# Gate blocks of a hybrid encoder layer computed before attention, in pairs with seven block products for eight

## The chip, the cores and the metric

The kernel runs on one core of a Trainium2 chip. A core has five engines that work beside one another, each through its own queue in order: PE (TensorE, matrix products into the accumulators in PSUM), ACT (ScalarE), DVE (VectorE), POOL (GpSimd) and SP, which here issues most transfers between DRAM and the on-chip memory SBUF. The metric is the time of one execution on the chip in microseconds (us); the number to compare is the median of several runs. For the kernel before it is 1957.97 us (three runs, 1956.46 to 1958.05).

## What is computed

One layer of a streaming encoder, for 1024 prompt tokens and 8 x 16 sample tokens together (1152 columns, `NT`). Cut to what matters here:

```python
h = rms_norm(x, norm_g) * (1 + scale) + shift
proj = h @ w_in
q, k, v, z_att, z_ssd, xbc, dt_raw, gates = jnp.split(proj, IN_SPLITS, axis=-1)
...
att_branch = (o_att.reshape(b, s, ATT_WIDTH) * jax.nn.silu(z_att)) @ w_att_proj
...
y = (y + d_skip.astype(jnp.float32)[:, None] * xs_h).reshape(b, s, SSD_WIDTH).astype(x.dtype)
y = y * jax.nn.silu(z_ssd)
...
merged = jax.nn.sigmoid(g_att) * att_branch + jax.nn.sigmoid(g_ssd) * ssd_branch
out = x + gate * (merged @ w_out)
```

All data is float32. `h` is 1024 x 1152 with features on partitions: eight row blocks of 128 (`KT`). A *gate block* is 128 columns of `w_in` for `z_att` (8 blocks) or `z_ssd` (16 blocks) times `h`, followed by a SiLU.

## The kernel before, in words

**Products.** Each float32 operand is split into a rounded high part and the rest (ACT copies to `fp32r`, DVE subtracts, lines 334 and 335 for weights), and a product is three passes: high by high, high by low, low by high. `dense` (line 427, its matmuls on lines 442, 443 and 445) makes one block of 128 outputs in three groups of 384 tokens: 8 row blocks x 3 passes x 3 groups = 72 matmuls of 128x384. `dense_tok` (506 to 508) makes the q, k and v of two heads with tokens on partitions: 9 token tiles of 24 matmuls, 128x384 each. The two accumulators of the pool `psd` (tile `d` in the profile) take turns in both. The attention and scan arithmetic itself runs in small float32 matmuls on other lines.

**Start.** Eight input blocks come in, `h` is normalised and split block by block (for each `k`: ACT lines 646, 651 and 655, DVE lines 633, 642, 643 and 658), and the first gate block is accumulated as each row block of `h` arrives (line 665). Row block `k` of `h` before its split (`ht[k]`) is freed at once.

**Attention.** Eight units of two heads. The dense work of unit u is `dense_tok`, and then the gate block of unit u+1 (line 924). Beside it run, as generators, a `prelude` (q and k are normalised on POOL, lines 960 to 964, and turned by PE, lines 984 and 1000, in three parts: tiles 0 to 3, 4 to 7, 8), and the attention of the unit before (`prompt`: scores on line 1122, DVE 1036, ACT 1031, turns 1043, products with v 1066; `sample`: 1175 to 1212). One buffer `Q` holds the raw q and k of a unit; it is free for the next unit once the third part of the prelude has been turned on line 1000. A token tile's accumulator is read by ACT on 931 and 933, into `Q`, and by DVE on 934.

**Scan (SSD).** Sixteen pairs of heads, p. The dense work of a pair is a convolution block (`conv_gen`), its gate block z (lines 1423 and 1424 read the accumulator), and for ten pairs (`GATED`) a merge gate block (line 1355). Every fourth pair has two convolution blocks more. The scan's own chain (lines 1453 to 1616) runs beside it; the dense work may be two pairs ahead (`AHEAD`).

**Tail.** Merge gates that are left, the two branch projections, the merge and the output projection.

**Order of the work.** Generators of dense work and of the rest are interleaved by `run`: for each piece of dense work its cost times a ratio (0.95 in attention, 0.5 elsewhere) is credit that the rest may spend, and `pause` holds a generator back by a planned time. The instructions so emitted are put into the engines' queues by a scheduler that may take a later instruction when an earlier one is not ready in its own model of time; what is wrapped in `late` stays behind the instruction emitted before it on its engine. At run time each queue is in order.

Of the kernel before, what the change touches and what calls it, by code (L numbers as in the profile page):

```python
# [12 lines left out]
P = 128  # L13
# [18 lines left out]
GATED = (0, 1, 2, 4, 5, 6, 8, 9, 10, 13)  # L32
BIG = -1e30
# [5 lines left out]
FCOLS = COLS - RCOLS - QCOLS - VCOLS  # L39
# [82 lines left out]
def trunk_kernel(ctx: ExitStack, tc: tile.TileContext, h):  # L122
# [12 lines left out]

    class Part:
# [15 lines left out]
    qpart, vpart = Part("q", QCOLS, "left"), Part("v", VCOLS, "right")  # L152
    qarena, varena = qpart.arena, vpart.arena
    q_phase, v_phase = qpart.phase, vpart.phase
    ctx.callback(qpart.close)
    ctx.callback(vpart.close)

    uid = [0]

    def nm(s):  # L160
        uid[0] += 1
        return f"{s}{uid[0]}"
# [40 lines left out]
    Z0 = fixed[0] + 2 * 1024  # L203
    XW = 3 * 288 + 2 * 256
    L_RAW = arena.set_layout(fixed[0], [("raw", 2, 1024)])
    L_ATT = arena.set_layout(Z0, [("Q", 1, 16 * P), ("T", 5, NT), ("S", 10, 640), ("U", 2, 640), ("K", 4, 512), ("q", 1, 256), ("d", 1, 256),
                                  ("k", 1, 128), ("p", 1, 128), ("n", 2, 36 + 3 * 16), ("t", 6, 14)])
    L_ATT["Z"] = L_ATT["T"][2:]
    L_SSD = arena.set_layout(Z0, [("X", 1, XW), ("R", 2, 1184), ("t", 8, 36), ("pad", 1, 576), ("T", 9, NT), ("Y", 1, 1184), ("H", 1, 1024),
                                  ("g", 3, G3)])  # L210
    L_HEAD = dict(L_SSD, T=[x for x in L_SSD["T"] if x[0] + x[1] <= Z0 + 7 * NT])
    L_START = arena.set_layout(Z0, [("T", 11, NT), ("ada", 5, 1024), ("e", 2, 256)])
    L_TAIL = arena.set_layout(Z0, [("T", 15, NT)])
    L_SM = arena.set_layout(Z0 + 15 * NT, [("e", 2, 384)])
# [3 lines left out]
    L_WA = rarena.set_layout(W0, [("w", 2, 1024)])  # L218
# [7 lines left out]
    L_VT = varena.set_layout(0, [("T", 5, 1184)])  # L226
    v_open = [False]

    def alloc(lay, tag, cols, cold=None):
# [12 lines left out]
        if lay is L_W3 or lay is L_W7 or lay is L_VT or lay is L_VA:  # L242
            return Buf(varena, varena.alloc(lay, tag, cols), cols)
        if lay is L_H or lay is L_W or lay is L_WA or lay is L_QR or lay is L_ST:
            return Buf(rarena, rarena.alloc(lay, tag, cols, cold), cols)
# [6 lines left out]
        return Buf(arena, arena.alloc(lay, tag, cols), cols)  # L252

    q_phase("start", F32)
# [14 lines left out]
    x0_ = Z0  # L269
    xv = []  # L270
    for w in (288, 288, 288, 256, 256):
        xv.append(base[:, x0_:x0_ + w])
        x0_ += w
    dt, acs, dtw, dec, decs = xv

# [10 lines left out]
    gate_d = drp.tile([16, P, NT], F32, name="gate_d")  # L286

# [28 lines left out]
    def w_split(i, keep=lambda x: x, cold=None):  # L316

        n = len(jobs[i])
        if n == 4:
            return w_split_last(i, keep)  # L320
        if i not in wsplit:
            lay = L_W3 if n == 3 else L_WA if 0 < i < jobs_att[0] else L_W
# [17 lines left out]
    def w_split_last(i, keep):  # L340
# [6 lines left out]
        if j == 3:  # L347
            row = alloc(L_WA, "w", 1024)
# [68 lines left out]
    job(h["wall"][0])  # L417
    for u in range(NU - 1):
        job(*(h["wall"][1 + 4 * u + i] for i in range(3)))
        job(h["wall"][4 + 4 * u])  # L420
    job(*(h["wlast"][i] for i in range(4)))
    jobs_att = [len(jobs)]
    for x in [h["wall"][i] for i in range(29, 85)] + [h["watt"][i] for i in range(8)] + [h["wssd"][i] for i in range(16)] \
# [3 lines left out]
    def dense(ops, evict, nk=KT, outs=1, last=False, wide=False, order=(0, 1, 2), other=False):  # L427
# [9 lines left out]
        def mm(ps, o, g, k, parts=(0, 1)):  # L437
# [3 lines left out]
            if 0 in parts:  # L441
                nc.tensor.matmul(ps, hi.r[:, wc], kh.r[:, tok], start=k == 0, stop=False)  # L442
                nc.tensor.matmul(ps, hi.r[:, wc], kl.r[:, tok], start=False, stop=False)  # L443
            if 1 in parts:
                nc.tensor.matmul(ps, lo.r[:, wc], kh.r[:, tok], start=False, stop=k == nk - 1)  # L445

        for o in range(outs):
# [21 lines left out]
            for g in order:  # L469
                if g == 2 and att_left[0] == 0:  # L470
# [16 lines left out]
    def dense_tok(evict):  # L487
# [5 lines left out]
        for t in range(9):  # L493

            ps = pg(n) if i == 1 and t == 2 else psd.tile([P, n], F32, tag="d", name=nm("d"))
# [22 lines left out]

    ct_ = alloc(L_START, "e", 256)
    dma(ct_.ap, h["cT"])  # L520
# [1404 lines left out]
```

## Time and profile before

| what | value |
|---|---|
| median of three runs | 1957.97 us (1956.46 to 1958.05) |
| span of the profiled execution | 1955.7 us |
| PE busy | 1938.3 us, 99% of the span |
| DVE, ACT, POOL busy | 1168.5, 776.4, 323.5 us |
| HBM traffic | 192.70 MB read, 43.66 MB written |

The span is from the first to the last instruction; the runs' times are 0.8 to 2.3 us above it, for what lies around it. In a row of the profile stand the line of the kernel, the engine, the operation, what it writes and reads with its shape, and a count; then the busy time, the mean length of one, and the idle time before it with what ended it. In a row of the timeline stand start and length in us first. A matmul's length contains the one behind it in the pipeline, so for PE the distance from start to start is the price of one.

### The profile page before, as it was taken

The numbers are of one execution on the slowest core, as the hardware profiler recorded it, in microseconds if no ns is written. First come the engines' busy times: TensorE is split into PE (matmuls) and PEld (weight loads), VectorE is DVE, ScalarE is ACT, GpSimd is POOL, SyncE is SP. The second block draws the span as 40 slices with busy tenths as digits, with TensorE's granted clock in tenths as the row PEclk, the third lists the DMA queues.
The fourth block names the chain that finished last, engine by engine and source line by source line (L and its number), as shares of the span: only waits on it lengthen the run. The fifth ranks groups of instructions, "written<-read, shape, count | busy, mean of one in ns | idle before, by whom it ended". The sixth has DMA issues, their size and how long they took to land.

```text
span 1955.7 us, 35068 instructions
## 1 busy us (share of the span) xinstructions
PE 1938.3 (99%) x14091; PEld 1859.4 (95%) x14091; DVE 1168.5 (60%) x2441; ACT 776.4 (40%) x1589; POOL 323.5 (17%) x624
## 2 busy tenths in 40 slices
PE   7999999999999999999999999999999999999999
PEld 5999999899998999999999999999999999999999
DVE  7455555556555765757566666576674334777732
ACT  8444444445444557344454434345351301111200
POOL 0312213122131201212212221122212100000000
PEclk9999999999999999999999999999999999999999
DMA  9124244232432325433333333332337642331241
GB/s 367 60 81 131 86 132 131 90 122 88 131 112 96 112 88 160 128 112 110 95 132 129 106 103 114 117 118 91 117 118 291 234 140 92 104 104 56 86 143 52
DMA packets 81209, 238.62 MB, mean 122 GB/s; under 512 B 14284, under 2 KB 15320, under 8 KB 81048
## 3 DMA queue, kind: packets, MB, share of 16 engines
q1 hardware_dynamic: 72088, 207.74, 32.7%
q0 software_dynamic: 8960, 28.65, 3.8%
q8 instruction: 111, 1.82, 0.4%
q14 instruction: 50, 0.41, 0.1%
HBM read 192.70 MB, written 43.66 MB: 121 GB/s over the span
## 4 chain that ended last, share of the span: by engine, by line
PE 96%; DVE 1%; ACT 1%; DMA 1%; issue 0%; SPq 0%
PE d L442 13%; PE d L443 13%; PE d L445 13%; PE s L442 5%; PE s L445 5%; PE s L443 5%; PE d L508 5%; PE d L506 5%; PE d L507 5%; PE g L1043 3%; PE g L1066 3%; PE g L1553 2%; PE s L1122 2%; PE g L1526 1%; PE g L1573 1%; PE g L1122 1%
## 5 line engine op out<-in xcount | busy, mean ns | idle before, releaser
L442 PE MATMUL d<-rarena 128*128 128x384 f32 x1520 | 517.4, 340 | 0.3 <-ACT arena L1355 0.3
L445 PE MATMUL d<-rarena 128*128 128x384 f32 x1520 | 511.4, 336 | 0.0
L443 PE MATMUL d<-rarena 128*128 128x384 f32 x1520 | 511.0, 336 | 0.0
L442 PEld LDWEIGHTS d<-rarena 128*128 128x128 f32 x1520 | 285.6, 188 | 4.6 <-issue 2.3
L443 PEld LDWEIGHTS d<-rarena 128*128 128x128 f32 x1520 | 285.6, 188 | 2.8 <-issue 2.4
L445 PEld LDWEIGHTS d<-rarena 128*128 128x128 f32 x1520 | 285.5, 188 | 1.1 <-issue 0.9
L334 ACT ACTIVATE rarena<-arena 128x1024 fp32r<-128x1024 f32 x92 | 97.5, 1060 | 314.1 <-PE s L443 226.2
L442 PE MATMUL s<-rarena 128*128 128x384 f32 x640 | 216.7, 339 | 0.0
L443 PE MATMUL s<-rarena 128*128 128x384 f32 x640 | 214.2, 335 | 0.0
L445 PE MATMUL s<-rarena 128*128 128x384 f32 x640 | 214.1, 334 | 0.0
L508 PE MATMUL d<-va_att,rarena 128*128 128x384 f32 (+1 forms) x559 | 195.0, 349 | 0.0
L506 PE MATMUL d<-va_att,rarena 128*128 128x384 f32 (+1 forms) x559 | 193.9, 347 | 0.0
L507 PE MATMUL d<-va_att,rarena 128*128 128x384 f32 (+1 forms) x559 | 191.0, 342 | 0.0
L335 DVE TENSOR_TENSOR rarena<-arena,rarena 128x1024 fp32r<-128x1024 f32 x92 | 113.2, 1230 | 82.7 <-ACT rarena L334 82.4
L1031 ACT ACTIVATE arena<-arena 128x640 f32<-128x640 f32 (+2 forms) x144 | 101.4, 706 | 138.0 <-DVE arena L1140 99.7
L442 PEld LDWEIGHTS s<-rarena 128*128 128x128 f32 x640 | 120.3, 188 | 1.0 <-issue 1.0
L443 PEld LDWEIGHTS s<-rarena 128*128 128x128 f32 x640 | 120.3, 188 | 0.0
L445 PEld LDWEIGHTS s<-rarena 128*128 128x128 f32 x640 | 120.1, 188 | 0.0
L508 PEld LDWEIGHTS d<-va_att,rarena 128*128 128x128 f32 x559 | 105.5, 189 | 3.9 <-issue 2.7
L1263 DVE SCALAR_TENSOR_TENSOR arena<-arena 128x1176 f32<-128x1176 f32 x66 | 99.9, 1514 | 15.5 <-ACT arena L1260 14.2
L506 PEld LDWEIGHTS d<-va_att,rarena 128*128 128x128 f32 x559 | 105.2, 188 | 3.1 <-issue 1.2
L507 PEld LDWEIGHTS d<-va_att,rarena 128*128 128x128 f32 x559 | 105.2, 188 | 1.0 <-issue 0.4
(345 smaller groups left out, 3212.9 us busy)
## 6 DMA issues: line engine op xcount, KB each, us to landing
arena<-in_wall_dram SPq DMA_DIRECT2D x85, 512.0 KB, 3.9
arena<-in_kc_dram SPq DMA_DIRECT2D x64, 256.0 KB, 4.2
arena<-in_vc_dram SPq DMA_DIRECT2D x64, 256.0 KB, 3.4
arena<-acs_d SPq DMA_DIRECT2D x19, 576.0 KB, 3.8
gate_d<-arena POOLq DMA_DIRECT2D x48, 192.0 KB, 2.5
arena<-y_d SPq DMA_DIRECT2D x15, 576.0 KB, 5.6
arena<-in_wssd_dram SPq DMA_DIRECT2D x16, 512.0 KB, 4.1
arena<-in_wada_dram SPq DMA_DIRECT2D x15, 512.0 KB, 8.9
```

What stands on the lines that cost most here:

```text
L334: keep(nc.scalar.activation(hi.r[:, c], b.ap, AF.Copy))
L335: keep(nc.vector.tensor_tensor(lo.r[:, c], b.ap, hi.ap[:, c], ALU.subtract))
L442: nc.tensor.matmul(ps, hi.r[:, wc], kh.r[:, tok], start=k == 0, stop=False)
L443: nc.tensor.matmul(ps, hi.r[:, wc], kl.r[:, tok], start=False, stop=False)
L445: nc.tensor.matmul(ps, lo.r[:, wc], kh.r[:, tok], start=False, stop=k == nk - 1)
L506: nc.tensor.matmul(ps, kh.r[:, tok], wh, start=j == 0, stop=False)
L507: nc.tensor.matmul(ps, kh.r[:, tok], wl, start=False, stop=False)
L508: nc.tensor.matmul(ps, kl.r[:, tok], wh, start=False, stop=j == KT - 1)
L1031: nc.scalar.activation(p, p, AF.Exp, bias=sm_[:, 4 + e:5 + e], scale=-1.0, accum_out=sm_[:, 6 + e:7 + e])
L1043: nc.tensor.transpose(ps[:, s * P:(s + 1) * P], p[:, (j + s) * P:(j + s + 1) * P], ident)
L1122: late(nc.tensor.matmul(banks[k][e][:, o:o + w], x.r[hs, qs], y.r[hs, kk], start=i == 0, stop=i == 2))
L1263: nc.vector.scalar_tensor_tensor(yc, r.ap[:, j:j + n], w4[:, i, j:j + 1], yc, ALU.mult, ALU.add)
```

## The change

Seventeen gate blocks (all eight of attention, and those of the scan pairs in `EARLY`) are computed between the start and attention, stored in DRAM (`z_d`), and loaded where they are used. Blocks 0, 1 and 16 are plain. Blocks 2 to 15 are done as seven pairs: two blocks of outputs by two halves of the contraction (even and odd row blocks of `h`) by two halves of the tokens (576 each) are a 2 x 2 block product, made with seven products in Winograd's form of Strassen's identity. The sums of blocks of `h` are made once on POOL, in place (`t_sum`), the sums of blocks of weights for each pair on POOL (`w_form`); both are then split on ACT and DVE. A product is 4 row blocks x 2 groups of 288 tokens x 3 passes. The outputs are summed partly in PSUM, partly by DVE. The memory is cut anew (a pool of 16 slots during this phase, then the arena of attention and scan over the same place). In attention `dense_tok` of unit u+1 follows that of unit u; the ratio there is 1.27. The scan pairs in `EARLY` have no z block of their own.

```diff
+EARLY = (0, 1, 2, 4, 5, 6, 8, 9, 10)
+NZ = 2
+NPR = 7
+TH = NT // 2
+MH = TH // 2
...
+    def t_sum(i, part):
+        a, b = (x.ap.rearrange("p (h c) -> p h c", c=TH) for x in (ht[2 * i], ht[2 * i + 1]))
+        if part == 0:
+            late(nc.gpsimd.tensor_tensor(a[:, 0], a[:, 1], a[:, 0], ALU.subtract))
+            late(nc.gpsimd.tensor_tensor(a[:, 1], b[:, 1], a[:, 1], ALU.subtract))
+        else:
+            late(nc.gpsimd.tensor_tensor(b[:, 1], b[:, 1], a[:, 0], ALU.subtract))
+            late(nc.gpsimd.tensor_tensor(b[:, 0], b[:, 0], b[:, 1], ALU.subtract))
+    def t_split(w, i):
+        x = ht.pop(2 * i + w)
+        hi, lo = thi[w][i], tlo[w][i] = [slots.alloc(F32R) for _ in range(2)]
+        late(nc.scalar.activation(hi.r, x.ap, AF.Copy))
+        late(nc.vector.tensor_tensor(lo.r, x.ap, hi.ap, ALU.subtract))
+        x.free()
+    FORMS = ("P1", "P5", "P7", "P6", "P2", "P4", "P3")
...
+    def w_form():
...
+        tt = lambda out, a, b, op: late(nc.gpsimd.tensor_tensor(out, a, b, op))
+        if f == "P1":
+            tt(t1, part(i1, 0), part(i1, 1), ALU.add)
+            tt(t2, t1, part(i0, 0), ALU.subtract)
+            tt(part(i1, 0), part(i0, 0), part(i1, 0), ALU.subtract)
...
+        late(nc.scalar.activation(v3(w.r[:, hi]), x, AF.Copy))
+        late(nc.vector.tensor_tensor(v3(w.r[:, lo]), x, v3(w.ap[:, hi]), ALU.subtract))
+        if f == "P5":
+            tt(t1, part(i0, 1), t2, ALU.subtract)
...
+        for j, (n, f) in enumerate(seq):
+            while len(forms) < min(j + 4, len(seq)):
+                w_form()
...
+            for i in range(KT // 2):
+                mh, ml, o = mv(i)
+                wh, wl = (w.r[:, c + i * P:c + (i + 1) * P] for c in (0, 512))
+                for g in range(2):
+                    tok = slice(o + g * MH, o + (g + 1) * MH)
+                    late(nc.tensor.matmul(bank[g], wh, mh[:, tok], start=fresh and i == 0, stop=False,
+                                          skip_group_check=not fresh))
...
+            elif f == "P6":
...
+                add(u2.ap, D_, s["p1"].ap)
+                s.pop("p1").free()
+                add(u3.ap, C_, u2.ap)
+                x = o2.ap[:, TH:]
+                add(x, B_, u3.ap)
+                u3.free()
+                silu(x, [v3(x)])
...
     for k in range(KT):
...
-            if 2 < k < 6:
-                w_low2(k - 3)
+            if k == 4:
+                late(nc.vector.tensor_tensor(wsplit[1][1].r, b.ap, wsplit[1][0].ap, ALU.subtract))
...
-        ht.pop(k).free()
...
+        if k % 2:
+            t_sum(k // 2, 0)
+            t_sum(k // 2, 1)
...
+    todo = [0, 1, 2, None, (0, 0), (0, 1), (0, 2), (0, 3), None, (1, 0)]
+    for j, _ in enumerate(dense(hops, ev_z(z[1], late), third=True)):
+        if j % 2 and todo:
+            x = todo.pop(0)
+            if x is None:
+                w_form()
+            elif isinstance(x, int):
+                ev_z(z[0], late)(0, x, groups[x], first[x])
...
+            else:
+                t_split(*x)
...
+    pairs()
+    z = alloc(L_ATT, "T", NT)
+    for i in range(NZ + 2 * NPR, nz):
+        for j, _ in enumerate(dense(hops, ev_z(z))):
+            if j in (6, 9, 12):
+                w_next(i - NPR)
+        dma(z_d[i], z.ap)
...
     def attention(u):
...
             qk = yield from walloc(lay, "Q", 16 * P)
             v = yield from walloc(lay, big, NT)
             nb = yield from walloc(lay, "n", 84)
+            z = zs[u] = yield from walloc(lay, big, NT)
+            dma(z.ap, z_d[u])
...
-                return
-            z = zs[u + 1] = yield from walloc(lay, "Z" if u + 1 == NU - 1 else "T", NT)
-            yield from dense(hops, ev_z(z))
...
-        return dense_gen(), [prelude()], [prompt(), sample()], 0.95
+        return dense_gen(), [prelude()], [prompt(), sample()], 1.27
...
+            if p in EARLY:
+                st["go"] = True
+                if p % PPG == 0:
+                    yield from conv_gen(p, lay, res)
+                if p in GATED:
+                    yield from gate_dense()
+                return
...
+            if p in EARLY:
+                z = yield from walloc(lay, "T", NT)
+                dma(z.ap, z_d[NU + EARLY.index(p)])
```

More of the change, by code (lines that the diff above doesn't have):

```diff
@@ L251, in alloc @@
                     pass
-        return Buf(arena, arena.alloc(lay, tag, cols), cols)
+        of = arena if lay is L_RAW else marena
+        return Buf(of, of.alloc(lay, tag, cols), cols)
+    slots.open()
     q_phase("start", F32)
```

314 lines of the change are left out of this document (226 added, 88 removed).

## The prediction

> **What bounds the kernel now.** I read the page first: its span, the busy time of the engines, the clock, and the chain that ended last.
>
> ```profile
> span 1955.7 us, 35068 instructions
> ...
> PE 1938.3 (99%) x14091; PEld 1859.4 (95%) x14091; DVE 1168.5 (60%) x2441; ACT 776.4 (40%) x1589; POOL 323.5 (17%) x624
> ...
> PEclk9999999999999999999999999999999999999999
> ...
> PE 96%; DVE 1%; ACT 1%; DMA 1%; issue 0%; SPq 0%
> ```
>
> PE is busy from end to end at its full clock, and 96% of the chain is PE. So the time is what PE has to do, and everything else is hidden behind it. Then the windows of 50 us, to see how much room the other engines leave where work is moved (columns: window, its length, PE, PEld, DVE, ACT, POOL busy, clock, DMA share, GB/s).
>
> ```profile
> 100.00:150.00 50.00, 50.00 (x426) 44.85 (x426) 28.70 (x100) 22.75 (x62) 7.72 (x14) 1.00 0.27 88
> 650.00:700.00 50.00, 50.00 (x457) 44.73 (x456) 39.95 (x108) 26.69 (x66) 11.29 (x32) 1.00 0.36 120
> 750.00:800.00 50.00, 48.25 (x347) 47.36 (x346) 36.85 (x64) 31.25 (x72) 9.68 (x17) 1.00 0.43 132
> 1000.00:1050.00 50.00, 50.00 (x356) 49.69 (x355) 32.26 (x52) 27.68 (x62) 9.63 (x18) 1.00 0.39 130
> ```
>
> The reader should see that PE stays full even in the second, where DVE is at 80%, and that only the third has a hole (1.75 us).
>
> **The products: minus 20.1.** What a matmul costs is the distance from start to start. The timeline of PE gives it for 384 columns (18 from the first to the second row) and for 256 (four of them up to the next row).
>
> ```profile
> 1702.06 0.33 PE L442 MATMUL d<-rarena 128*128 128x384 f32 x1
> ...
> 1705.18 0.33 PE L442 MATMUL d<-rarena 128*128 128x384 f32 x1
> ...
> 783.61 0.63 PE L1598 MATMUL g<-rarena 128*128 128x256 f32 x4
> 784.08 0.34 PE L442 MATMUL d<-rarena 128*128 128x384 f32 x1
> ```
>
> 3.12 / 18 = 0.1733 us for 384 and 0.47 / 4 = 0.1175 for 256. On the line between them 288 columns cost 0.1175 + 32 x 0.0558 / 128 = 0.1315, an estimate. Two plain blocks are 144 x 0.1733 = 24.96; seven products are 7 x 24 x 0.1315 = 22.09. A pair saves 2.87, seven pairs 20.1. That is less than an eighth of 7 x 24.96 because a narrower matmul pays the same fixed share. Blocks 0, 1 and 16 only change their place.
>
> **Does PE stay full while the pairs run?** Per pair PE needs 22.1 us. The prices of the others:
>
> ```profile
> L335 DVE TENSOR_TENSOR rarena<-arena,rarena 128x1024 fp32r<-128x1024 f32 x92 | 113.2, 1230 | 82.7 <-ACT rarena L334 82.4
> L1646 DVE TENSOR_TENSOR rarena<-arena,rarena 128x1152 fp32r<-128x1152 f32 x26 | 34.8, 1352 | 6.9 <-ACT rarena L1644 6.7
> L801 DVE SCALAR_TENSOR_TENSOR arena<-arena,d 128x384 f32<-128x384 f32 x21 | 11.6, 550 | 29.7 <-ACT arena L800 29.7
> L964 POOL TENSOR_TENSOR arena<-arena 128x1024 f32<-128x1024 f32 x16 | 31.6, 1972 | 1.3
> L964 POOL TENSOR_TENSOR arena<-arena 128x256 f32<-128x256 f32 x8 | 5.1, 639 | 0.6
> arena<-in_wall_dram SPq DMA_DIRECT2D x85, 512.0 KB, 3.9
> ```
>
> DVE: seven low parts of 512 columns (0.62 each, half of L335), five sums and four SiLU ends of 576 (0.83 each by L801): 11.8. POOL: four sums of 512, each 639 + 1333 / 3 = 1.08: 4.3. The weight forms are made three products (9.5 us) ahead, the raw weights land in 3.9. Every one of these hides; I take 0, and 1 us for the recut of memory and the first products after it (0 to 4). The stores and loads of the blocks are 17 of 0.59 MB each way on SP, at a DMA share under 0.45 in the windows: 0. In a scan pair SP waits for z's buffer with the next weights queued behind, and ACT and PE behind those; two loaded buffers cover that. If they did not, it would be 3.9 per pair.
>
> **The start: plus 12.** Here the sums of `h` are added. PE and DVE between the first split and the last:
>
> ```profile
> 28.83 1.36 DVE L658 TENSOR_TENSOR rarena<-arena,rarena 128x1152 fp32r<-128x1152 f32 x1 [0.50 <-ACT arena L651]
> ...
> 53.31 0.29 DVE L642 TENSOR_TENSOR arena<-arena 128x128 f32<-128x128 f32 x1 [0.88 <-ACT arena L625]
> ...
> 55.92 1.36 DVE L658 TENSOR_TENSOR rarena<-arena,rarena 128x1152 fp32r<-128x1152 f32 x1 [0.72 <-ACT arena L651]
> ...
> 43.05 0.51 PE L506 MATMUL d<-va_att,rarena 128*128 128x384 f32 x2
> ...
> 63.89 0.38 ACT L931 ACTIVATE arena<-g 128x256 f32<-128x256 f32 x1
> ```
>
> DVE works through `h` until 57.3, with little idle. PE would wait for it, but from 43.05 on it fills up with token tiles of unit 0; three of them (72 matmuls) are ready at 63.9. After the change block 1 is that filling, also 72 matmuls, so blocks 0 and 1 could be done at 63.9 and P1 (24 x 0.1315) at 67.1. P5 then needs the first sums of `h` split. For DVE: 57.3, less two weight splits of 1.23 that go, plus three SiLU ends (1.65), four splits (5.4) and two weight forms (1.2): 63.1. That is 4.0 ahead of PE, if POOL leaves DVE alone. POOL has 16 sums of 576 (639 + 1333 x 320 / 768 = 1.19 each) and three of 512 to do by then: 22.3. Does a POOL sum stop DVE? Two meetings in one unit's prelude say different things.
>
> ```profile
> 241.83 2.90 POOL L291 TENSOR_TENSOR arena<-arena 128x16 f32<-128x16 f32 x1
> 242.28 1.23 DVE L335 TENSOR_TENSOR va_att<-arena,va_att 128x1024 fp32r<-128x1024 f32 x1 [0.98 <-ACT va_att L334]
> ...
> 248.06 1.91 POOL L964 TENSOR_TENSOR arena<-arena 128x1024 f32<-128x1024 f32 x1
> 248.29 2.75 DVE L335 TENSOR_TENSOR va_att<-arena,va_att 128x1024 fp32r<-128x1024 f32 x1 [1.36 <-ACT va_att L334]
> ```
>
> Beside POOL's long operation on 16 columns DVE's subtraction took its usual 1.23; beside the one that streams 1024 columns it took 2.75, and the two together 2.98 where one after the other is 3.14. The sums stream like the second, so they and DVE take turns, with 0.16 shared each time. Of the 22.3, then, 19 x 0.16 = 3.0 is shared, 1.65 lies beside the SiLU ends (one input from PSUM), 1.6 in the idle time shown, and 4.0 in DVE's lead: 12.0 are left, and PE waits that long. Bounds: 0, if the sums are as harmless as the first meeting, and 18.3, if nothing but the lead hides them. No gain: before 63.9 PE has other work.
>
> The Trainium skill (SBUF — State Buffer, "Who interferes with whom") has a rule against this change: a DVE instruction with two inputs in SBUF and a GpSimd instruction that reads SBUF exclude each other for the whole instruction. The second meeting agrees (2.75 for 1.23), the first does not (1.23). By the rule in full nothing would be shared and the term would be 15.0.
>
> **Attention: plus 3, minus 2.** A unit loses 12.5 us of dense work that lay between its token tiles and the next unit's. Those may not be evicted before the last turn of the prelude, on L1000, frees `Q`.
>
> ```profile
> 239.32 0.34 PE L506 MATMUL d<-va_att,rarena 128*128 128x384 f32 x1
> ...
> 241.40 0.20 POOL L960 TENSOR_SCALAR arena<-arena 128x16 f32<-128x16 f32 x1 [20.22 <-DVE arena L937]
> ...
> 247.20 1.06 ACT L334 ACTIVATE va_att<-arena 128x1024 fp32r<-128x1024 f32 x1 [1.22 <-DMA arena<-in_wall_dram]
> ...
> 249.59 3.43 PE g L1066 x60
> 253.02 1.23 PE g L1202 x40
> ...
> 254.24 0.61 POOL L964 TENSOR_TENSOR arena<-arena 128x256 f32<-128x256 f32 x1
> ...
> 264.12 0.38 PE L1000 MATMUL g<-arena 128*128 128x128 f32 x2
> ...
> 330.04 3.43 PE g L1066 x60
> ```
>
> The first row begins token tile 8; POOL's chain for tiles 4 to 7 and for tile 8 ends at 254.85, so for 15.5 us L1000 cannot run. In the kernel before, the gate block filled this, up to 264.12. After: tile 8 and, into the two free accumulators, tiles 0 and 1 of the next unit are 72 x 0.1733 = 12.5, the turns 1.0; the unit before still owes 3.43 + 1.23 at that place. 18.2 against 15.5: covered. Without that last part 2.0 are missing. A second limit: the third part of the next weights is copied at 247.20 and subtracted by 251.0 (the 2.75 above); tile 0 gets through five of eight row blocks before, at 239.3 + 4.2 + 2.6 = 246.1, a hole of 4.9 less what the unit before fills. I take 0.5 for each of seven boundaries, rounded to 3; bounds 0 and 34. The engines have room: 28.70 per 50 is 46.2 of DVE in a unit of 80.45 (249.59 to 330.04); less 2.9 for the gate block, in 68, it is 64%. A gain: each return from attention to dense work costs PE time.
>
> ```profile
> 245.58 0.27 PE L1043 MATMUL g<-arena 128*128 128x128 f32 x1
> 245.61 0.42 PE L442 MATMUL d<-rarena 128*128 128x384 f32 x1
> 245.87 0.34 PE L443 MATMUL d<-rarena 128*128 128x384 f32 x1
> ```
>
> 0.26 instead of 0.17. With three quarters of the dense work I estimate three returns fewer per unit: 8 x 3 x 0.09 = 2 (0 to 4).
>
> **Scan: plus 1.**
>
> ```profile
> 1010.52 2.12 PE g L1553 x36
> 1056.54 2.12 PE g L1553 x36
> ```
>
> A gated pair takes 46.0, of which three blocks are 37.4. Without z it is 33.5, and DVE (32.26 per 50, so 29.7, less 2.9) is at 80%, where 650 to 700 was full. Bounds 0 and nine pairs at the hole of 750 to 800: 9 x 33.5 x 1.75 / 50 = 10.6.
>
> **Sum:** -20.1 + 1 + 12 + 3 - 2 + 1 = -5. The profiled span, 1955.7, becomes 1950.7; the runs lie 0.8 to 2.3 above it, and the median of 1957.97 becomes 1953.
>
> **The rivals.** *Start unhurt*: the sums on POOL run in DVE's shadow as at 241.83; then 1953 - 12 = 1941. For it: one of the two meetings. *Boundaries run dry*: with the ratio at 1.27 a unit's attention is over before its boundary, PE stands for 2.5 to 3 us in each of seven, some 18 in all: 1971, slower. It decides from 0.7 us a boundary. For it: 15.5 us of POOL that nothing shortens; against: the order lets later tiles go first. By the Trainium skill (TensorE: Matmul & The Clock Gate, Part 1) a window of about 3.4 us without work also halves PE's clock; no window here has a granted clock below 1.00. *Scan bound by DVE*: 10 more, 1963. *No cheaper matmul*: if 288 columns take 0.1733, seven products cost 29.1, a pair 4.2 more than now: 1953 + 20.1 + 29.1 = 2002; against it stands the row at 256.
>
> **Numbers.** About 0.2% (3.9 us) is what a measurement here can tell from no change. The forecast has 0.45 (own range 1946 to 1960: 0.24 faster, 0.19 same, 0.02 slower); start unhurt 0.20; boundaries dry 0.18; scan 0.10 (0.04 same, 0.06 slower); no cheaper matmul 0.03; something better than all this 0.04. Faster 0.48, same 0.23, slower 0.29. The range, 1938 to 1972, leaves out the last two and the outer parts of the second and third.
>
> **What would show it.** Right: matmuls of 128x288 0.13 apart; DVE's splits stretched beside POOL's sums and PE idle for about 12 us before P5; no idle above 1 us between token tiles; PE full in the scan. Wrong: a start no longer than now, holes before each L1000, or PE waiting for DVE in the scan.

## The result, and the profile after

The kernel after takes 1977.01 us (median of four runs, 1976.15 to 1979.02), the kernel before on the same chip 1958.01 (1956.46 to 1959.59): a ratio of 1.01, with a 95% interval of 1.0086 to 1.0115. It is 19 us slower, where 5 us faster was forecast; 1977 also lies outside the range of 1938 to 1972.

The page of after, the lines that answer to those of before:

```profile
span 1974.4 us, 35771 instructions
...
PE 1941.3 (98%) x14259; PEld 1847.7 (94%) x14259; DVE 1220.4 (62%) x2533; ACT 799.8 (41%) x1639; POOL 396.1 (20%) x668
...
PE 91%; DVE 3%; ACT 2%; issue 1%; DMA 1%; SPq 0%; POOL 0%; ACTq 0%; DVEq 0%; POOLq 0%
```

PE still carries the chain, but 91% of it instead of 96%: DVE has 3% of it instead of 1%, ACT 2% instead of 1%, so their work now ends more of PE's waits. The windows tell where (columns as in the prediction):

```profile
50.00:100.00 50.00, 42.70 (x274) 40.45 (x266) 44.67 (x45) 28.84 (x46) 29.41 (x17) 0.97 0.17 56
150.00:200.00 50.00, 50.00 (x378) 50.00 (x377) 25.34 (x44) 16.64 (x32) 10.27 (x8) 1.00 0.33 112
450.00:500.00 50.00, 50.00 (x475) 45.65 (x478) 27.05 (x89) 23.01 (x52) 15.47 (x24) 1.00 0.33 101
1300.00:1350.00 50.00, 45.22 (x341) 43.74 (x341) 44.74 (x76) 25.07 (x57) 12.61 (x21) 0.97 0.53 162
```

The pairs (second row) and attention (third) show a full PE; the start and one place in the scan do not. But a full PE is not PE at its best, since a matmul's length contains waiting in the pipeline. So the loss is counted otherwise. Give each matmul a price, which is a distance from start to start: for the wide ones what it is among their like (0.1733 for 384 columns, 0.19 for 416, and 0.133 for 288, from after, since before had none), for all others what their line and shape had on average in before. Call **surplus** what passes, up to the last matmul, beyond the sum of these prices. The sum fell from 1896.0 to 1877.7 us: the products do save 18.3. The surplus rose from 55.5 to 92.5:

| stage | before | after | forecast of the difference |
|---|---|---|---|
| start, up to the first token tile of attention (before: up to 100 us) | 12.3 | 28.8 | +13 |
| attention, up to the last product with v | 26.6 | 40.1 | +1 |
| scan and tail | 16.5 | 23.6 | +1 |

-18.3 + 16.5 + 13.5 + 7.1 = 18.8; the spans differ by 18.7. There are three places, then, one for each stage.

**Start.** These are DVE's and then POOL's rows of the same stretch in after's timeline:

```profile
47.68 1.35 DVE L680 TENSOR_TENSOR m<-m,m 128x1152 f32<-128x1152 f32 x1
49.13 1.33 DVE L689 TENSOR_TENSOR m<-m,arena 128x128 f32<-128x128 f32 x1
50.49 1.46 DVE L690 TENSOR_TENSOR m<-m,arena 128x128 f32<-128x128 f32 x1
```

```profile
47.90 2.41 POOL L769 TENSOR_TENSOR m<-m,m 128x576 f32<-128x576 f32 x1 [1.56 <-DVE rarena L705]
50.39 1.41 POOL L770 TENSOR_TENSOR m<-m 128x576 f32<-128x576 f32 x1
```

DVE's operations on 128 columns took 0.29 in before. Here the first ends at 50.46, when POOL's sum (47.90 + 2.41 = 50.31) is over, the second at 51.95, when the next sum is (51.80). And the first sum took 2.41 instead of 1.41 because DVE's own operation held it until 49.03. Here they take turns by whole instructions. In PE's timeline this is what comes of it:

```profile
75.81 0.29 PE L867 MATMUL g<-rarena 128*128 128x288 f32 x1
...
78.99 0.29 PE L867 MATMUL g<-m,rarena 128*128 128x288 f32 x1
...
82.88 0.40 PE L870 MATMUL g<-m,rarena 128*128 128x288 f32 x1 [3.46 <-DVE rarena L803]
```

P1 is 24 matmuls in 3.18 us: 0.1325 each, so the estimate of 0.1315 held. P1 was forecast to begin at 63.9 and be over at 67.1; it begins at 75.8, and P5 then stands 3.46 more.

**Attention.** The last turn of the prelude runs once a unit. PE's timeline of before (the turn ahead of this one is at 264.12, in the prediction, so they are 80.45 apart), then of after:

```profile
344.57 0.38 PE L1000 MATMUL g<-arena 128*128 128x128 f32 x2
```

```profile
369.04 0.38 PE L1223 MATMUL g<-arena,ma_att 128*128 128x128 f32 x2
...
438.52 0.38 PE L1223 MATMUL g<-arena,ma_att 128*128 128x128 f32 x2
```

These are 69.48 apart. A unit lost a gate block of 72 x 0.1733 = 12.48 and became only 10.97 shorter. A pair costs 7 x 24 x 0.133 = 22.3, so 11.2 for each of its blocks: more than a block was worth where it stood.

**Scan.** There is one hole, at the twelfth pair. It has 7.3 us of the surplus, with the slow clock behind it (told of at the end). PE's timeline of after:

```profile
1338.75 2.13 PE L1787 MATMUL g<-ma_att,va_ssd 128*64 128x128 f32 x30 [2.02 <-DVE ma_att L1689]
1343.64 0.44 PE L481 MATMUL d<-rarena 128*128 128x384 f32 x1 [2.76 <-DVE ma_att L1654]
```

### The profile page after: what moved, and what is told of

It reads as the page before. It is cut to its first block, busy times and chain, and to the rows that moved or that the text cites. A ratio compares the mean times of both kernels' runs of the same rounds, so it can differ in the third digit from the quotient of the medians.

```text
span 1974.4 us, 35771 instructions
## 1 busy us (share of the span) xinstructions
PE 1941.3 (98%) x14259; PEld 1847.7 (94%) x14259; DVE 1220.4 (62%) x2533; ACT 799.8 (41%) x1639; POOL 396.1 (20%) x668
## 4 chain that ended last, share of the span: by engine, by line
PE 91%; DVE 3%; ACT 2%; issue 1%; DMA 1%; SPq 0%; POOL 0%; ACTq 0%; DVEq 0%; POOLq 0%
PE d L481 11%; PE d L484 11%; PE d L482 11%; PE d L545 5%; PE d L547 5%; PE d L546 5%; PE s L481 5%; PE s L484 5%; PE s L482 5%; PE g L1266 3%; PE g L1289 3%; PE s L1345 2%; PE g L1345 1%; PE g L1787 1%; PE g L870 1%
## 5 line engine op out<-in xcount | busy, mean ns | idle before, releaser
L481 PE MATMUL d<-rarena 128*128 128x384 f32 x1248 | 425.5, 341 | 3.9 <-DVE ma_att L1654 2.8
L484 PE MATMUL d<-rarena 128*128 128x384 f32 x1248 | 419.8, 337 | 0.0
L482 PE MATMUL d<-rarena 128*128 128x384 f32 x1248 | 419.7, 336 | 0.0
L481 PEld LDWEIGHTS d<-rarena 128*128 128x128 f32 x1248 | 235.4, 189 | 6.4 <-DVE ma_att L1654 3.0
L484 PEld LDWEIGHTS d<-rarena 128*128 128x128 f32 x1248 | 234.8, 188 | 1.1 <-issue 1.0
L482 PEld LDWEIGHTS d<-rarena 128*128 128x128 f32 x1248 | 235.4, 189 | 0.3
L481 PE MATMUL s<-rarena 128*128 128x384 f32 x576 | 196.4, 341 | 1.4 <-DVE va_start L993 1.4
L545 PE MATMUL d<-va_att,rarena 128*128 128x384 f32 (+1 forms) x567 | 196.9, 348 | 0.0
L369 ACT ACTIVATE rarena<-arena 128x1024 fp32r<-128x1024 f32 x77 | 81.5, 1059 | 283.5 <-PE s L482 197.6
L547 PE MATMUL d<-va_att,rarena 128*128 128x384 f32 (+1 forms) x567 | 195.2, 344 | 0.0
L546 PE MATMUL d<-va_att,rarena 128*128 128x384 f32 (+1 forms) x567 | 194.1, 342 | 0.1
L484 PE MATMUL s<-rarena 128*128 128x384 f32 x576 | 193.4, 336 | 0.0
L482 PE MATMUL s<-rarena 128*128 128x384 f32 x576 | 192.7, 335 | 0.0
L1254 ACT ACTIVATE ma_att<-ma_att 128x640 f32<-128x640 f32 (+2 forms) x144 | 101.7, 709 | 105.4 <-DVE ma_att L1363 80.5
L370 DVE TENSOR_TENSOR rarena<-arena,rarena 128x1024 fp32r<-128x1024 f32 x77 | 95.2, 1237 | 56.4 <-ACT rarena L369 55.9
L481 PEld LDWEIGHTS s<-rarena 128*128 128x128 f32 x576 | 108.3, 188 | 4.5 <-issue 2.5
L545 PEld LDWEIGHTS d<-va_att,rarena 128*128 128x128 f32 x567 | 107.1, 189 | 4.7 <-issue 3.6
L546 PEld LDWEIGHTS d<-va_att,rarena 128*128 128x128 f32 x567 | 106.7, 188 | 3.0 <-issue 2.4
L547 PEld LDWEIGHTS d<-va_att,rarena 128*128 128x128 f32 x567 | 106.6, 188 | 2.3
L484 PEld LDWEIGHTS s<-rarena 128*128 128x128 f32 x576 | 108.2, 188 | 0.7 <-issue 0.6
L482 PEld LDWEIGHTS s<-rarena 128*128 128x128 f32 x576 | 108.3, 188 | 0.0
L1683 ACT ACTIVATE ma_att<-ma_att 128x128 f32<-128x128 f32 x234 | 72.3, 390 | 88.0 <-DMA ma_att<-acs_d 75.3
```

The lines of the kernel that those rows point to most:

```text
L369: keep(nc.scalar.activation(hi.r[:, c], b.ap, AF.Copy))
L370: keep(nc.vector.tensor_tensor(lo.r[:, c], b.ap, hi.ap[:, c], ALU.subtract))
L481: keep(nc.tensor.matmul(ps, hi.r[:, wc], kh.r[:, tok], start=k == 0, stop=False))
L482: keep(nc.tensor.matmul(ps, hi.r[:, wc], kl.r[:, tok], start=False, stop=False))
L484: keep(nc.tensor.matmul(ps, lo.r[:, wc], kh.r[:, tok], start=False, stop=k == nk - 1))
L545: nc.tensor.matmul(ps, kh.r[:, tok], wh, start=j == 0, stop=False)
```

## The experiments

The table has every run's median, its ratio to before and the three surpluses of its profiled execution. That execution is one of the runs and can lie some us off their median (e10 3.9 below, e13 3.7 and e16 3.6 above), so a surplus is to be compared with other surpluses, not with the medians.

| run | median us | ratio (95%) | products | start | attention | scan, tail |
|---|---|---|---|---|---|---|
| after | 1977.01 | 1.01 (1.0086 to 1.0115) | -18.3 | 28.8 | 40.1 | 23.6 |
| e1_no_t_sums | 1960.63 | 1.0019 (1.001 to 1.0029) | -18.3 | 15.3 | 40.1 | 22.6 |
| e4_plain_ahead | 1983.05 | 1.0133 (1.0118 to 1.0148) | 0 | 15.7 | 41.7 | 24.0 |
| e7_start | 1973.11 | 1.0079 (1.0061 to 1.0097) | -18.3 | 28.6 | 47.8 | 16.3 |
| e9_start_late | 1969.14 | 1.0067 (1.0054 to 1.008) | -18.3 | 24.0 | 40.1 | 21.2 |
| e13_dve_sums | 1968.47 | 1.0061 (1.0048 to 1.0075) | -18.3 | 21.6 | 40.1 | 26.9 |
| e2_ratio_095 | 1986.63 | 1.0149 (1.0132 to 1.0166) | -18.3 | 30.3 | 50.3 | 24.9 |
| e12_ratio_19 | 1974.84 | 1.0089 (1.0076 to 1.0102) | -18.3 | 29.5 | 39.5 | 22.9 |
| e5_q_halves | 2009.53 | 1.0267 (1.025 to 1.0283) | -18.3 | 30.3 | 70.6 | 26.9 |
| e8_all | 1999.43 | 1.0217 (1.02 to 1.0233) | -18.3 | 25.8 | 71.7 | 18.0 |
| e3_early_13 | 1985.56 | 1.0148 (1.0133 to 1.0164) | -18.3 | 29.1 | 40.1 | 31.8 |
| e6_scan_ratio | 1975.86 | 1.0098 (1.0082 to 1.0115) | -18.3 | 29.2 | 46.5 | 16.8 |
| e10_att_home | 1968.98 | 1.0055 (1.0041 to 1.0069) | -10.4 | 24.1 | 26.0 | 23.8 |
| e14_home_dve | 1960.64 | 1.0018 (1.001 to 1.0027) | -10.4 | 22.1 | 26.0 | 23.8 |
| e15_home5_dve | 1955.46 | 0.9995 (0.9986 to 1.0004) | -13.0 | 21.8 | 26.0 | 17.8 |
| e16_home5_pipe | 1950.80 | 0.9971 (0.9961 to 0.9982) | -13.0 | 18.2 | 26.0 | 21.5 |
| e17_home6_pipe | 1968.80 | 1.0056 (1.0043 to 1.007) | -15.7 | 18.0 | 26.0 | 40.4 |

### The move alone: e4_plain_ahead

```diff
-NZ = 2
-NPR = 7
+NZ = 16
+NPR = 0
...
```

> All seventeen blocks ahead of attention as plain blocks of 72 matmuls, no sums, no pairs: the move alone. Theory (a pair in the steady state is 2.6 us cheaper than two plain blocks, seven give 18.3; the start loses about 14 without the sums): 1977 + 18 - 14 = 1981, that is some 23 slower than before: the move costs in attention 13, in the scan 7.5, in the start 2 to 3. Rival (the loss is in the pairs, the move is free): 1958, as before.

Measured: 1983.05. With PE's work as in before, attention's surplus is 41.7 for 26.6 and the scan's 24.0 for 16.5. So the loss in both comes with the move of the gate blocks, not with the identity. Against this run the pairs bring 6 us by the medians, and 7 by the profiled executions: 18.3, less the 13.1 that the start pays for them (28.8 for 15.7), and 2.0 less surplus in the two other stages.

### The start: e1, e7, e9, e13

e1_no_t_sums leaves out the two calls of `t_sum`.

> Left out: the sixteen sums of blocks of h, so the pairs are computed from unsummed blocks. Theory (POOL's sums and DVE take turns in the start): DVE's short operations on 128 columns go back from 1.33 to 0.29 us, the first block ends at about 62.3 as before instead of 69.1, the stall of 3.5 in P5 goes; about 13 us less than after, 1964. Rival (the start is longer because DVE and ACT have more splits to do, POOL does no harm): 2 us less at most, 1975.

Measured: 1960.63, and the start's surplus falls from 28.8 to 15.3. DVE in e1's timeline, the same operations with no sum beside them:

```profile
47.08 0.29 DVE L689 TENSOR_TENSOR va_start<-m,arena 128x128 f32<-128x128 f32 x1
47.41 0.29 DVE L690 TENSOR_TENSOR va_start<-va_start,arena 128x128 f32<-128x128 f32 x1
```

Back at 0.29, and the first block ends at 59.4. The sixteen sums cost 13.5; what else the start has gained in work costs 3.0.

e7_start puts the same sums, in the program, behind the loop and beside a second plain block:

```diff
-        if k % 2:
-            t_sum(k // 2, 0)
-            t_sum(k // 2, 1)
...
+    todo = [0, 1, 2, (0, 0, 0), (0, 0), (1, 0, 0), (0, 1), (2, 0, 0), (0, 2), (3, 0, 0), (0, 3)]
...
-        return dense_gen(), [prelude()], [main()], 0.5
+        return dense_gen(), [prelude()], [main()], 0.75
```

> As the run with the ratio 0.75 in the scan, and the sums of h are moved behind the loop of the start, beside two plain blocks instead of one (pair 12 is added to the early ones, so the seven pairs stay and one plain block is still last). Theory (DVE and POOL take turns only while both are wanted; in the loop of the start DVE sets the pace, beside a plain block it has room): the first block ends near 60 to 62 instead of 69.1, no stall of over 1 us up to the second pair; 12 us less than the run with 0.75 alone, 1958. Rival (the sums cost the same wherever they are, or P6 now waits for them): within 4 us of the run with 0.75 alone.

Measured: 1973.11, start 28.6: the start has won nothing. POOL's timeline in e7 gives the first reason:

```profile
29.78 1.41 POOL L766 TENSOR_TENSOR m<-m 128x576 f32<-128x576 f32 x1 [29.34 <-DVE rarena L705]
...
64.00 1.43 POOL L766 TENSOR_TENSOR va_start<-va_start 128x576 f32<-128x576 f32 x1 [8.47 <-DVE rarena L705]
```

POOL's queue was empty, so half of the sums ran as soon as their rows of `h` were there, inside the loop as in after; the first block ends at 67.2 instead of 69.1. What that gave was lost again at 73.10, where PE stood 4.91 until DVE had done the end of a plain block. A later place in the program delays nothing on an engine that has nothing else to do. e9_start_late therefore gives them something to wait for:

```diff
+                late(nc.gpsimd.tensor_scalar(small.ap[:, :1], z[0].ap[:, :1], 1.0, 0.0, ALU.mult, ALU.add))
...
-        return dense_gen(), [prelude()], [main()], 0.5
+        return dense_gen(), [prelude()], [main()], 0.75 if p >= PPG else 0.5
```

> As the run with the sums behind the loop, but now they really wait: a small POOL operation that reads the first block's finished part stands ahead of them in POOL's queue (in the run before this one POOL took them up as soon as h was there, inside the loop, since its queue was empty). The ratio of the scan is 0.75 from pair 4 on, 0.5 before. Theory (in the loop of the start DVE sets the pace and every turn that POOL takes lengthens it; beside a plain block DVE has room): the first block ends at 59 to 60, the second pair starts with no stall over 1 us, the start loses 3 more than before's instead of 16.6; with the hole of the scan gone too, 1977 - 12 - 7 = 1958. Rival (the sums cost the same wherever they are): 1970.

Measured: 1969.14, as the rival had it, and start 24.0: 4.8 of the 13.5 came back, not 12. The first block now ends at 58.1, but the sums have become a chain of their own on POOL:

```profile
59.59 1.39 POOL L766 TENSOR_TENSOR m<-m 128x576 f32<-128x576 f32 x1
61.06 2.27 POOL L767 TENSOR_TENSOR m<-m,m 128x576 f32<-128x576 f32 x1
...
93.97 1.74 POOL L770 TENSOR_TENSOR va_start<-va_start 128x576 f32<-128x576 f32 x1
```

That is 36 us for sixteen sums and four of weights, with the splits waiting behind them. e13_dve_sums hands the same late sums to DVE (`nc.gpsimd` becomes `nc.vector` in `t_sum`; 0.75 from pair 1 on).

> As the run with the late sums, but DVE does them (sixteen of 576 columns at about 0.7 us), and 0.75 in the scan from pair 1 on. Theory (late on POOL the start still lost 11.6 more than before's, because POOL's chain of sums, 35 us with its turns, set the splits and the second block's ends behind them; DVE does them in 11 us beside 24 us of plain blocks): the start loses 3 more than before's, 9 us less than that run, 1960. Rival (it is the number of operations on the way to P5 and P6, on whichever engine): within 3 us of it, 1966 to 1972.

Measured: 1968.47, start 21.6. The median is within 1 us of e9's, as the rival had it. In the profiled execution the start is 2.4 better, but the scan has two holes (26.9); how many of the other executions have them is not known. The runs e15 and e16, below, show part of what the start still pays.

### Attention: e2, e12, e5, e8

e2_ratio_095 sets the ratio 1.27 to 0.95, e12_ratio_19 to 1.9; nothing else.

> The ratio of attention back at 0.95. Theory (a gate block among attention cost 11.0 us of PE, not 12.5, because small products that follow a wide one partly hide in it; with fewer wide ones they follow one another, at any ratio): within 3 us of after, a unit stays at 69 to 70. Rival (1.27 bunches the small products; spread out again they cost what they cost before): a unit comes down from 69.5 to 68.0, 10 us less, 1967. If attention then has no room left it is longer instead, over 1980.

> The ratio of attention at 1.9, after otherwise; 0.95 gave 10 us more. Theory (the loss is that of a unit with three quarters of the dense work, once the attention chain keeps up): units stay at 69 to 70, 1974 to 1980. Rival (the ratio of 1.27 is what bunches or delays the small products): units at 68, 1967.

Measured: 1986.63 and 1974.84. With 0.95 attention is longer still (surplus 50.3): most of its units take 71.4, and PE stands 0.4 and 0.6 us for DVE at most of their ends. With 1.9 nothing changes. L1223 in e12's timeline, 69.48 apart again:

```profile
369.69 0.38 PE L1223 MATMUL g<-arena,ma_att 128*128 128x128 f32 x2
...
439.17 0.38 PE L1223 MATMUL g<-arena,ma_att 128*128 128x128 f32 x2
```

e5_q_halves takes away the wait for `Q`:

```diff
-    L_ATT = marena.set_layout(Z0, [("Q", 1, 16 * P), ("T", 5, NT), ...
+    L_ATT = marena.set_layout(Z0, [("Q", 2, 8 * P), ("q8", 1, NT), ("T", 4, NT), ...
...
-                c = qk.ap[:, 2 * (t % 8) * P:2 * (t % 8 + 1) * P]
+                i = t // 4
+                if i not in st["qk"]:
+                    st["qk"][i] = yield from (walloc(lay, "Q", 8 * P) if i < 2 else walloc(lay, "q8", 2 * P))
+                c = st["qk"][i].ap[:, 2 * (t % 4) * P:2 * (t % 4 + 1) * P]
```

> Q in two halves of four token tiles and a small buffer for tile 8, each freed once it is turned, so the next unit's token tiles need not wait for the last turn of the prelude in the order of the work; z is loaded later, one buffer less for it. Theory now (attention loses 1.5 us per unit because the order of the work has no dense work to give while Q is taken, so that attention's small products are put one after another without wide ones between): a unit comes down from 69.5 to about 68, 12 us less, 1965, if the scan does not change. Rival (the loss belongs to a unit with three quarters of the dense work, whatever the order): within 3 us of after, 1974 to 1980.

Measured: 2009.53, a miss for both. From the first unit's last turn to the last unit's it is 511 us (306.95 to 818.20), where after has 491, and PE now stands in attention for 23 us in all, where after has 0.7. The longest of these waits is in unit 7's token tiles; PE's row of e5, then DVE's:

```profile
742.16 0.72 PE L545 MATMUL d<-va_att,rarena 128*128 128x416 f32 x1 [6.52 <-DVE ma_att L1160]
```

```profile
741.92 0.29 DVE L1160 COPY ma_att<-d 128x32 f32<-128x32 f32 x2 [4.26 <-DMA att_d<-ma_att]
```

L1160 empties an accumulator into a buffer `T`, and it had to wait until a store had freed one. The edit itself took one of the five `T` away. So this run does not tell what the wait for `Q` costs: the buffer and the wait were changed together, and no run takes them apart.

e8_all has the edits of e5, e6 and e7 together:

> The three edits together: Q in halves, 0.75 in the scan, sums of h behind the loop beside a second plain block. If the three losses are apart from one another, 1977 less 7, 12 and 12: 1946, which is faster than before. If attention's loss is inherent, 1958; if the losses are one another's cover, 1965 or more.

Measured: 1999.43, with attention's 71.7 as in e5: what e5 added there outweighs the rest, so the run does not tell whether the three losses are apart.

### The scan: e3, e6

e3_early_13 has 13 in place of 10 in `EARLY`.

> Pair 13 in place of pair 10 gets its gate block from DRAM, so pair 10 has three dense blocks again. Theory (the hole of 7.5 us at 1336 to 1344 is DVE falling behind ahead of the change of group, 44.7 busy in 50): hole gone, 1970. Rival (the loads on SP wait for a buffer held by z and block what is queued behind): the hole stays or moves to another pair, 1977.

Measured: 1985.56, a miss for the theory: the hole did not go, there are two (PE's timeline of e3). The rival was right that a hole moves, but it had 1977.

```profile
1261.76 3.64 PE L1787 MATMUL g<-ma_att 128*64 128x128 f32 x30 [5.33 <-issue]
...
1445.15 3.68 PE L1787 MATMUL g<-ma_att 128*64 128x128 f32 x32 [4.50 <-issue]
```

e6_scan_ratio lets the scan's own work be issued earlier beside the shorter dense work:

```diff
-        return dense_gen(), [prelude()], [main()], 0.5
+        return dense_gen(), [prelude()], [main()], 0.75
```

> The ratio of the scan pairs from 0.5 to 0.75, nothing else: each piece of dense work lets more of the scan's own work be issued beside it. Theory (with a block less per pair the scan's chain falls behind the dense work, which then runs out of buffers, and what is left of the chain stands alone: the hole of 7.5 us at 1336 to 1344): hole gone, 1970. Rival (DVE is at its limit around the change of group, whatever the order): 1977, the hole stays or moves, as it did with pair 13 in place of pair 10.

Measured: 1975.86. The scan's surplus is 16.8, before's 16.5: the hole was the order of the work, not DVE's limit. But 6.4 come back in the last unit of attention, whose rest is now issued with less dense work between, in short stalls (PE's timeline of e6):

```profile
833.94 0.66 PE L1266 MATMUL g<-arena,ma_att 128*128 128x128 f32 x4 [1.53 <-ACT ma_att L1534]
...
843.84 0.61 PE L1558 MATMUL g<-arena,ma_att 128*32 128x128 f32 x4 [1.98 <-ACT ma_att L1551]
```

### Attention as it was, pairs for the scan alone: e10, e14, e15, e16, e17

Here the gate blocks of units 1 to 7 stay between the units with the ratio 0.95; one block of attention and eleven (e15 and e16: thirteen, e17: fifteen) of the scan are computed ahead, eight (ten, twelve) of them in four (five, six) pairs. e10 has e9's late sums on POOL, the others e13's on DVE.

```diff
-    nz = NU + len(EARLY)
+    nz = 1 + len(EARLY)
...
+            z = zs[u + 1] = yield from walloc(lay, "Z" if u + 1 == NU - 1 else "T", NT)
+            yield from dense(hops, ev_z(z))
...
-        return dense_gen(), [prelude()], [prompt(), sample()], 1.27
+        return dense_gen(), [prelude()], [prompt(), sample()], 0.95
```

> Attention as it was before (its gate blocks between the units, ratio 0.95); only eleven gate blocks of the scan and the first one of attention are computed ahead, eight of them in four pairs; sums of h late and 0.75 in the scan from pair 4 on, as in the run beside it. Theory (a gate block moved out of attention gives 11 us, out of the scan the full 12.5, and a pair's block costs 11.2): units at 80.4 again, four pairs save 10.4, the start costs 3: 1950. Rival (attention's extra loss comes from elsewhere, such as the loads of z or the memory cut anew): units longer than 80.4, 1960 or more.

Measured: 1968.98. Its total is a miss, since the start still pays 11.8 more than before's and the scan 7.3; attention does what was expected, 80.45 a unit (322.49 and 402.94 in e10's timeline of PE):

```profile
322.49 0.38 PE L1247 MATMUL g<-arena,ma_att 128*128 128x128 f32 x2
...
402.94 0.38 PE L1247 MATMUL g<-arena,ma_att 128*128 128x128 f32 x2
```

So the recut memory and the phase ahead do not hurt attention; taking its blocks away does. The loads of z went with the blocks, all but one, but PE stands for only 0.7 us in the whole of after's attention, so the loads do not hold it up.

> Attention as before, four pairs of scan blocks, the sums late on DVE, 0.75 in the scan from pair 1 on. Terms: four pairs -10.4, start +3, scan +2 to +6, attention 0: 1949 to 1956, faster than before or the same. Rival (the start does not get cheaper): 1960.

> The same with five pairs, thirteen of the scan's sixteen gate blocks ahead, and a ratio of 1.0 in the scan. Theory: one pair more is worth 2.6: 1947 to 1954. Rival (with so little dense work per pair the scan is bound by DVE and its own chain): 1965 or more.

Measured: 1960.64, a miss at its rival's figure, and 1955.46, 1.5 us above what was expected. With the ratio 1.0 in the scan (0.6 in pair 0) e15's scan is at 17.8, though its pairs have still less dense work. What is left is in the start. PE's stalls in e15:

```profile
61.80 0.44 PE L484 MATMUL s<-rarena 128*128 128x384 f32 x1 [2.38 <-DVE va_start L994]
...
74.36 0.44 PE L484 MATMUL d<-rarena 128*128 128x384 f32 x1 [2.38 <-DVE va_start L994]
...
81.00 0.44 PE L484 MATMUL s<-rarena 128*128 128x384 f32 x1 [2.19 <-DVE va_start L994]
```

L994 is the end of a plain block, which frees its accumulator. At the second and third stall it stood in the queues behind splits that waited for sums (an ACT copy, then DVE); at the first it stood behind the split of a weight. e16_home5_pipe only changes the order:

```diff
-    todo = [0, 1, 2, (0, 0, 0), (0, 0), (1, 0, 0), (0, 1), (2, 0, 0), (0, 2), (3, 0, 0), (0, 3)]
+    todo = [0, 1, 2, (0, 0, 0), (1, 0, 0), (0, 0), (2, 0, 0), (), (0, 1), (3, 0, 0), (0, 2)]
...
```

> The five pairs, only the order in the start changed: each split of sums is issued after the next sums, and the ends of the plain blocks come between, not behind. Theory (the three stalls of 2.2 to 2.4 us at 59, 72 and 79 are the order in the in-order queues, not the work): two of the three go, 4 to 5 us less, 1951, faster than before. Rival (DVE simply has too much to do up to the second pair): stalls move to P5 and P6, 1955.

> The same with six pairs, fifteen of the scan's sixteen gate blocks ahead. Theory (each pair 2.6): 1948. Rival (the scan is then bound by DVE and its own chain, and the tail waits for it): 1960 or more.

Measured: 1950.80 for e16, a ratio of 0.9971 (0.9961 to 0.9982): faster than before by 6 us, or 0.3%. Two of the three stalls are gone (start 18.2); the first, behind the weight, is still there, 3.05 us at 62.63. e17 is 1968.80, a miss for its theory and on the rival's side: with fifteen of the sixteen gate blocks gone from the scan, PE stands beside its last pairs, and the clock falls to 0.80 (windows of e17):

```profile
1500.00:1550.00 50.00, 48.55 (x360) 47.46 (x360) 33.03 (x62) 20.66 (x39) 7.89 (x15) 1.00 0.71 247
1550.00:1600.00 50.00, 39.27 (x242) 33.94 (x241) 20.38 (x32) 6.58 (x7) 8.17 (x15) 0.80 0.75 258
```

## Why the prediction was wrong, point by point

The sum missed by 24 us: 1.8 of it in the products, 3.5 in the start, 12.5 in attention and 6.1 in the scan.

**The products** were right: 18.3 for 20.1, at 0.1325 to 0.133 a matmul.

**The start, +13,** had the right mechanism and was 3.5 short. e1 prices the sums at 13.5, where 12.0 was taken, and all the rest at 3.0, where 1 was taken. Each sum takes 1.28 to 1.41 where 1.19 was taken, and nothing is shared, as the rows at 49.13 and 50.49 show. The place was another one, too: PE was to wait for some 12 us ahead of P5, and waited there for 3.46; most of the loss had come before P1. The bounds of the sums, up to 18.3, held. By the Trainium skill (SBUF — State Buffer, "Who interferes with whom") a DVE instruction with two inputs in SBUF and a GpSimd instruction that reads SBUF exclude each other for the whole instruction. The trace agrees (1.33 for 0.29), and the 15.0 which that rule gave was as near to the 13.5 as the 12.0.

**Attention, "plus 3, minus 2",** is the step that failed, by 12.5. The plus was for boundaries that run dry, and that was right to be small: token tiles of the next unit run across them, and no stall of over 0.5 us is there. The minus was wrong in kind. It read the row at 245.61 (0.26 instead of 0.17) as the price of a return from narrow products to wide ones, and left out what the narrow product ahead of it saves: 245.58 to 245.61 is 0.03, where a turn among turns takes 0.11. Counted from PE's timeline over four units (264.12 to 585.92 before, 369.04 to 646.96 after): stretches of wide matmuls fell from 27 to 17 a unit, and the time that they took from 53.3 to 39.9, 0.9 more than the 12.5 of the block, so the gain of returns is there and larger than forecast. But the narrow products took 27.2 in before and 29.5 in after. PE stands nowhere in these units, and among its like a matmul costs what it did (a wide one 0.174 in both, a turn 0.111 and 0.113), so it is the order that costs. Now the narrow products follow one another, kind after kind. PE's timeline of after:

```profile
465.88 0.33 PE L547 MATMUL d<-va_att,rarena 128*128 128x384 f32 x1
466.14 1.53 PE L1289 MATMUL g<-ma_att 128*64 128x128 f32 x24
467.60 0.50 PE L1345 MATMUL s<-rarena 64*128 64x512 f32 x2
...
468.86 0.40 PE L1345 MATMUL g<-rarena 64*128 64x512 f32 x2
469.19 0.33 PE L1435 MATMUL g<-arena,ma_att 128*128 128x128 f32 x1
469.27 0.42 PE L545 MATMUL d<-va_att,rarena 128*128 128x384 f32 x1
```

There are three kinds in one stretch. Where the kind changes it takes 0.2 to 0.33 to the next start (24 products with v at 0.055 would be over by 467.46). Before, 20 turns a unit were followed by a wide matmul, at 0.03; after, 9. That the loss belongs to the blocks taken away is shown: the ratio (e12) and the kind of the blocks ahead (e4) leave it at 39.5 or more, and 26.0 returns with the blocks (e10, e14 to e17). That the changes of kind make it up is read from a count. All of attention has the same 3176 narrow products in e10 and in after; they take 218.6 us in e10 and 237.7 in after, and the wide ones behind them give 5.6 back, together 13.6 of the 14.1 by which the surpluses differ. In e10 218 of them are followed by a wide matmul and 100 by a narrow one of another kind; in after 150 and 138. No run changes the order alone.

**The scan, +1,** was inside its bounds (0 to 10.6) with 7.1, but as one hole of 7.3 and not as many small ones. The forecast priced it by DVE's load. e6, which changes the ratio alone, shows that the order of the work, with a ratio made for three blocks a pair, was the cause. The rival *Scan bound by DVE* was thus wrong in its reason.

**The rivals.** *Boundaries run dry* gave 1971 on the side where the result came out, but by stalls at the boundaries, which the trace does not have. No rival had the loss in it that decided: that a wide block between narrow products is worth less than its own matmuls.

## What to carry to other kernels

Price work that is to be moved by what its present neighbours lose without it, not by its own matmuls: a wide block among narrow products was worth 11.0 us here and the same block in the scan 12.5 (e6 has nine of them less and the surplus of before), and against 11.2 for the cheaper product only the second was a gain. When the share of one kind of work changes, the order that was tuned to the old share costs a good part of the saving: 7.1 us by the ratio 0.5 in the scan, 4.7 by the queue order in the start (e15 to e16), where the products saved 18.3 and 13.0. So look at the in-order queues before the engines' loads. An instruction placed later in the program is later only if its engine has something to do or to wait for until then.

## What was not expected of the hardware

The same stall in P5 (3.75 us from start to start, at 79) is followed by a full clock in one run and by half in another; windows of after and of e2:

```profile
82.90:86.00 3.10, 3.10 (x22) 2.96 (x23) 3.10 (x6) 0.78 (x2) 2.28 (x1) 1.00 0.00 0
...
1344.30:1347.30 3.00, 3.00 (x11) 3.00 (x11) 3.00 (x6) 0.00 (x0) 0.00 (x0) 0.50 0.81 329
```

```profile
82.90:86.00 3.10, 3.10 (x13) 3.10 (x14) 3.10 (x6) 0.78 (x2) 2.26 (x1) 0.50 0.00 0
```

22 matmuls at a clock of 1.00, against 13 at 0.50. After itself has a halved clock at 1344, behind the two pauses of 2.02 and 2.76 us shown under *Scan*, with 2.1 us of work between. So a pause of 2 to 4 us can cost more than its own length: nothing more in after's P5, 1.0 us in the second row (11 matmuls at 0.27 where 0.1733 is usual), and 9 matmuls of 288 columns, 1.2 us, in the window of e2 alone.

The traces show what came before each halving, if they are cut where the clock changes. In after the half clock lasts from 43.61 to 47.02, from 53.85 to 57.26 and from 1344.09 to 1347.50, 3.41 us each time. The rows below are stretches of this length, laid so that their borders fall on those changes; the first number behind the length is PE's busy time, the third from the right the clock. Windows of after, then of e2:

```profile
77.74:81.14 3.40, 1.68 (x13) 1.45 (x11) 3.40 (x3) 2.91 (x7) 1.54 (x1) 1.00 0.00 0
81.15:84.56 3.41, 1.68 (x12) 1.68 (x13) 3.41 (x6) 2.53 (x3) 1.59 (x1) 1.00 0.00 0
...
1340.68:1344.09 3.41, 0.65 (x7) 0.46 (x4) 3.41 (x6) 1.37 (x1) 1.48 (x3) 1.00 0.74 157
1344.09:1347.50 3.41, 3.41 (x12) 3.41 (x12) 3.41 (x7) 0.00 (x0) 0.00 (x0) 0.50 0.78 318
```

```profile
78.20:81.60 3.40, 1.18 (x9) 0.94 (x8) 3.40 (x2) 2.89 (x7) 1.07 (x1) 1.00 0.00 0
81.61:85.02 3.41, 2.14 (x9) 2.15 (x10) 3.41 (x6) 2.07 (x3) 2.05 (x1) 0.50 0.00 0
```

After's stall in P5 falls half into one stretch and half into the next; PE is busy for 1.68 us in each, and the clock stays. In e2 the same stall leaves 1.18 in the first, at 1344 the second pause leaves 0.65, and the clock halves at the next border. Over all eighteen traces, behind the first 17 us, 46 stretches at full clock have PE busy for less than 1.67 us, and each is followed by half clock; of the 43 between 1.67 and 2.25 us 12 are, and of all above that two. This is a count, and no run was made for it.

The Trainium skill (TensorE: Matmul & The Clock Gate, Part 1) has the clock decided by a window of about 3.4 us that runs free of the kernel. The stretches agree with that (3.41 us, and the same stall with and without a halving). But the prediction took the window to be one without any work, and here one was enough in which PE had worked for 1.18 of 3.40 us.
